# Two transformer layers with experts on one core: order of the first loads, norm factors as rows, scatters bounded to real rows, kept loads behind the first layer's only, one of two row sums moved to VectorE

## The chip, the cores and the metric

The kernel runs on one core of a Trainium2 chip. The metric is the device time of one execution in microseconds (us), lower is better. One execution was profiled; all rows below come from it. Engines are named as the profile names them: PE multiplies matrices (PEld is its weight load, which runs beside it), DVE, ACT and POOL work on elements, SP only issues DMAs here. A "q" behind the name (SPq, ACTq, POOLq) is that engine's own sequencer: the DMAs that it issues.

## The reference

Two layers of a decoder over T = 512 tokens of width D = 1024, fp32. Layer 0 mixes tokens by dilated window attention, layer 1 by stick-breaking attention (16 heads each). Behind each mixer stands a norm, a router that picks 2 of 16 experts for each token, the experts, and a second norm.

```python
for layer in range(DEPTH):
    mixed = mixer_dilated(x, ...) if layer == 0 else mixer_stick_breaking(x, ...)
    x = layer_norm(DEEPNORM_ALPHA * x + mixed, ln1_g[layer], ln1_b[layer])
    ffn = moe_ffn(x, router_w, router_b, exp_w_gate[layer], exp_w_up[layer], exp_w_down[layer])
    x = layer_norm(DEEPNORM_ALPHA * x + ffn, ln2_g[layer], ln2_b[layer])
```

`moe_ffn` gathers the tokens of each expert, computes `(silu(x @ w_gate) * (x @ w_up)) @ w_down`, scales each row by the token's gate and adds it back to the token's row. 512 tokens times 2 are 1024 rows for 16 experts, 64 an expert on average.

## The kernel before

**Products.** Every fp32 product is done as three products of high and low parts (`mm3`, L151 to L153). `split` makes the parts: ACT copies the high one (L143), DVE subtracts for the low one (L145). Weights come from HBM as raw fp32 on SP's queue, in chunks in the order of use, and are split before PE reads them. The tile framework orders the instructions of each engine by a timeline of its own, so an edit at one place can move instructions at others.

**Start.** x is four row blocks of 128 tokens (`xres<-x`, L375). `rows_to_T` (L331) transposes a block on PE, eight 128x128 transposes, and splits it. The first projection multiplies blocks 0 and 1 first, then 2 and 3 (`rest`). `load_router` (L393 to L408) loads the router's weights, its bias, and the factors g and b of the first norm of both layers by six DMAs on ACT's queue; the four of the factors (L400) go element by element, since element k*128+p of a vector must land on partition p. DVE multiplies them into the router's weights (`rwg`, L404) and sums them (L405).

**Kept parts.** While layer 0 runs, the weights of layer 1's projections are split ahead (`split_ahead`, L269) and their parts written back to HBM by POOL (`kept<-raw`, L276). `parts_of` loads them again by SP (`whi<-kept`, `wlo<-kept`, L281). Each such load waits for the expert weights' load issued last (`at["recent"][-1]`) and for the reload of the row blocks behind the experts (`at["read"]`). In layer 1, `prefetch()` queues loads of expert weights ahead from head 12 on (of 16), and the last kept chunk (kept_121, the last quarter of the output projection) stands behind them.

**Experts.** Each expert has 96 slots (CAP). POOL gathers the rows of its tokens (`gather`, L1091, with a bounds check: slots without a token are skipped). `expert_up` and `expert_down` make Y (96 x 1024), and POOL adds it to the tokens' rows in HBM by a scatter (L1127) into `x2_d`. An empty slot is scattered too, to a spare row behind the 512 real ones, which are written once at the start of the layer (`x2_d[T:]`, L1286). Scatters go one behind the other, as each adds to the same tensor. Of the 16 experts 14 are scattered; the last two are added on PE by one-hot products (L1261). SP loads the weights of the experts (1 MB gate, 1 MB up, 1 MB down each) with at most two chunks in flight (`OUTSTANDING`, L227).

**End of a layer.** When the last scatter has landed, SP reads the 512 rows back (`xres<-x_d`, L1222), PE brings each block into PSUM (`take`, L1236) and adds the last two experts, and the norm follows: for each block ACT sums both halves of a row (L1268, a copy with an accumulated sum), DVE makes the mean (L1269), ACT sums squares (L1271), DVE scales and shifts (L1273, L1278). SP's conditional for overflowing experts stands at L1241.

Of the kernel before, what the change touches and what calls it, by code (L numbers as in the profile page):

```python
# [11 lines left out]
F32 = mybir.dt.float32  # L12
# [9 lines left out]
P = 128  # L22
# [48 lines left out]
def trunk_kernel(ctx, tc, A, out):  # L71
# [19 lines left out]
    def bank(pl):  # L91
        return pl.tile([P, 512], F32, name="bank")
# [109 lines left out]
    RM = (2, 4, 5, 2)  # L202
    RY = 2

    def load(i):

        srcs, kind, j = chunks[i]
        if i in raws or kind == "b":
            return
        k = srcs[0].shape[1]  # L210
        if kind == "a":
            raw = rawp.tile([P, 2048], F32, name="raw0")
            raws[i] = [raw[:, :1024], raw[:, 1024:]]
            for half, t in enumerate(raws[i]):
                load_part(t, srcs, half, 2)
            return
        if j < RY:
            pl = pools["ry"]
        else:
            j, ring = (j - RY) % sum(RM), 0  # L220
            while j >= RM[ring]:
                j, ring = j - RM[ring], ring + 1
            pl = pools["rm", ring] if ring else rawp
        raw = pl.tile([P, 2048], F32, name=f"raw{j}" if pl is rawp else "raw") if hasattr(pl, "tile") else             pl[j // 2][:, j % 2]
        recent = at["recent"]
        for part, src in enumerate(srcs):
            ins = sp.dma_start(raw.rearrange("p (s k c) -> p s k c", k=k, s=len(srcs))[:, part], src).ins  # L227

            for before in (at["after"], recent[-OUTSTANDING] if len(recent) >= OUTSTANDING else None):
                if before is not None:  # L230
                    after(ins, before)
        recent.append(ins)
        raws[i] = (raw, k, len(srcs) == 2)
# [35 lines left out]
    def split_ahead():  # L269

        if coming:
            i, part = coming.pop(0)
            raw = rawp.tile([P, 2048], F32, name="raw1")
            load_part(raw[:, 1024:1536], chunks[i][0], part, 4)
            split(raw[:, :512].bitcast(F32R), raw[:, 512:1024].bitcast(F32R), raw[:, 1024:1536])
            pool.dma_start(kept[i][part], raw[:, :1024].rearrange("p (j c) -> p j c", j=2))  # L276

    def parts_of(i, half):
        parts = [splp.tile([P, 1024], F32R, name=f"w{x}") for x in ("hi", "lo")]
        for j, t in enumerate(parts):  # L280
            ins = sp.dma_start(t.bitcast(F32).rearrange("p (q c) -> p q c", q=2),  # L281
                               kept[i][2 * half:2 * half + 2, :, j].rearrange("q p c -> p q c")).ins
            for before in (at["recent"][-1], at["read"]):
                after(ins, before)
        return parts

# [83 lines left out]
    xS = [xp.tile([P, KT, T], F32R, name=f"xT{s}") for s in "hl"]  # L370
    xres = xp.tile([P, 4, D], F32, name="xres")
    for n in range(4):
        if n == 2:
            load_to(1)
        sp.dma_start(xres[:, n, :], x[n * P:(n + 1) * P, :])  # L375

    rest = []
    for n in range(4):
        if n < 2:
            at["begun"] = rows_to_T(*xS, xres[:, n, :], n, streams=True)  # L380
        else:
            rest.append(lambda n=n: rows_to_T(*xS, xres[:, n, :], n, streams=True))


    rb = const.tile([P, NE], F32, name="rb")
# [4 lines left out]
    def load_router():  # L390
        tmp = xp.tile([P, 5, KT * NE], F32, name="tmp", tag="Ol")
        rw = tmp[:, 0].rearrange("p (k e) -> p k e", k=KT)
        gbs = tmp[:, 1, :4 * KT].rearrange("p (j k) -> p j k", j=4)  # L393
        sums = tmp[:, 4, :4 * NE].rearrange("p (j e) -> p j e", j=4)
        with tc.issue_after(at["begun"]):
            act.dma_start(rw, A["router_w"].rearrange("(k p) e -> p k e", p=P))
            act.dma_start(rb, bass.AP(tensor=A["router_b"].tensor, offset=A["router_b"].offset, ap=[[0, P], [1, NE]]))
            for l in range(2):
                for i, name in enumerate(("ln1_g", "ln1_b")):
                    act.dma_start(gbs[:, 2 * l + i], A[name][l].rearrange("(k p) -> p k", p=P))  # L400
        for l in range(2):
            w2 = [rwg[l], tmp[:, 2].rearrange("p (k e) -> p k e", k=KT)]
            for i in range(2):
                tt(w2[i], rw, gbs[:, 2 * l + i, :, None].to_broadcast([P, KT, NE]), op=ALU.mult)  # L404
                dve.tensor_reduce(sums[:, 2 * l + i], w2[i].rearrange("p k e -> p e k"), axis=AX.X, op=ALU.add)  # L405
        ps = bank(psC)[:, :4 * NE]
        pe.matmul(ps, lhsT=ones_r.bitcast(F32), rhs=tmp[:, 4, :4 * NE], start=True, stop=True)
        dve.tensor_copy(gsum.rearrange("p l i e -> p (l i e)"), ps)  # L408
# [699 lines left out]
    def expert_down(mp, hs, Y, wd, gate, x2_d=None, row=None):  # L1108

        pt = bank(psC)[:, :2 * CAP].rearrange("p (k t) -> p k t", k=2)  # L1110
        for k in range(2):
            pe.transpose(pt[:, k, :], hs[:, k * P:(k + 1) * P], ident[:CAP, :CAP])
        hh = mp.tile([P, 2, CAP], F32R, name="hh")
        hl = mp.tile([P, 2, CAP], F32R, name="hl")
        split(hh, hl, pt)
        wd = wd()
        for c in range(2):
            ps = bank(psD)[:CAP]
            for k in range(2):
                mm3(ps, hh[:, k, :], hl[:, k, :], *wd(k, c * 512, (c + 1) * 512), k == 0, k == 1)  # L1120
            if row is None:
                split(*Y, ps, scale=gate, view=lambda t: t[:, c * 512:(c + 1) * 512])
            else:
                act.activation(Y[:, c * 512:(c + 1) * 512], ps, AF.Copy, scale=gate)  # L1124
        if row is None:
            return
        pool.indirect_dma_start(out=x2_d[:, :], out_offset=bass.IndirectOffsetOnAxis(ap=row, axis=0),  # L1127
                                in_=Y, in_offset=None, compute_op=ALU.add)

    def overflow(l, x1_d, x2_d, rt, X, Y, XX):  # L1130

# [33 lines left out]
    def post(l, x1, x2_d, last, done):  # L1165
        with ExitStack() as c:
# [79 lines left out]
            with ExitStack() as c2:  # L1246
                cp = open_pool(c2, f"cp{l}")

                act.activation(cp.tile([P, 1], F32, name="root"), spare1, AF.Sqrt)
                mv = cp.tile([P, 4, 6], F32, name="mv")  # L1250
                st = cp.tile([P, 4, 4], F32, name="st")
                junk = cp.tile([P, D], BF16, name="junk")
                halves = [slice(half * 512, half * 512 + 512) for half in range(2)]
                for n in range(4):
                    if n:
                        take(n)
                    ps, r = sums[n], xres[:, n, :]
                    for i, parts in enumerate(late):
                        for half, cs in enumerate(halves):
                            for j, t in enumerate(parts):  # L1260
                                ins = pe.matmul(ps[half], lhsT=holds[:, i, n * P:(n + 1) * P], rhs=t[:, cs], start=False,  # L1261
                                                stop=i * j == 1, skip_group_check=True).ins
                    if n == 0:
                        with tc.issue_after(ins):
                            load_to(at["load"] + 2)
                            split_to(at["split"] + 2)
                    for half, cs in enumerate(halves):
                        act.activation(junk[:, cs], ps[half], AF.Copy, accum_out=st[:, n, half:half + 1])  # L1268
                    stt(mv[:, n, 0:1], st[:, n, 0:1], st[:, n, 1:2], neg_d, op0=ALU.add, op1=ALU.mult)  # L1269
                    for half, cs in enumerate(halves):  # L1270
                        act.activation(junk[:, cs], ps[half], AF.Square, bias=mv[:, n, 0:1],  # L1271
                                       accum_out=st[:, n, 2 + half:3 + half])
                        stt(r[:, cs], ps[half], mv[:, n, 0:1], g_b[:, cs], op0=ALU.add, op1=ALU.mult)  # L1273
                    if n % 2:
                        tt(mv[:, n - 1:n + 1, 1], st[:, n - 1:n + 1, 2], st[:, n - 1:n + 1, 3], op=ALU.add)  # L1275
                        scale_of(mv[:, n - 1:n + 1], EPS / ALPHA ** 2)
                    for m in (n - 1, n) if n % 2 else ():
                        stt(xres[:, m, :], xres[:, m, :], mv[:, m, 3:4], b_b, op0=ALU.mult, op1=ALU.add)  # L1278
                        done(m, xres[:, m, :])
        return xres  # L1280

    def layer(l, attend, xTs, xres, done):
        last = []

        x2_d = dram.tile([T + P, D], F32, name=f"x2_d{l}")
        sp.dma_start(x2_d[T:], xres[:, 0])  # L1286

        def project_out(qd, Oh, Ol):
            def gen():
# [49 lines left out]
```

## Time and profile before

| | before |
|---|---|
| median of 3 runs (lowest to highest) | 1361.58 us (1356.65 to 1364.33) |
| the profiled execution | 1364.12 us, span 1362.3 us |
| mean granted TensorE clock | 0.954 |
| PE busy | 1247.7 us (92%) |
| DVE, ACT, POOL busy | 899.1, 859.0, 203.4 us |
| DMA moved | 289.60 MB, mean 213 GB/s |
| scatters `x_d<-Y,wr` | 28 issues |

The span is the time from the first to the last instruction, and 1.8 us of the execution lie around it. The page cuts the span into 40 slices of 34 us; a digit is the tenth of a slice that an engine is busy. PEclk is the granted clock of TensorE: 1.00 is the level of 2.4 GHz, 0.50 that of 1.2 GHz, and between them a stretch has some of each. Layer 0's first gathers stand at 654 us and its experts' last stretch at 765 to 821 us; layer 1's last stretch is at 1265 to 1318 us.

### The profile page before, as it was taken

The numbers are of one execution on the slowest core, as the hardware profiler recorded it, in microseconds if no ns is written. First come the engines' busy times: TensorE is split into PE (matmuls) and PEld (weight loads), VectorE is DVE, ScalarE is ACT, GpSimd is POOL, SyncE is SP. The second block draws the span as 40 slices with busy tenths as digits, with TensorE's granted clock in tenths as the row PEclk, the third lists the DMA queues.
The fourth block names the chain that finished last, engine by engine and source line by source line (L and its number), as shares of the span: only waits on it lengthen the run. The fifth ranks groups of instructions, "written<-read, shape, count | busy, mean of one in ns | idle before, by whom it ended". The sixth has DMA issues, their size and how long they took to land. (4 is left out here: it accounts for less than half of the span.)

```text
span 1362.3 us, 19699 instructions
## 1 busy us (share of the span) xinstructions
PE 1247.7 (92%) x6784; PEld 1022.9 (75%) x6784; DVE 899.1 (66%) x1620; ACT 859.0 (63%) x1538; POOL 203.4 (15%) x285
## 2 busy tenths in 40 slices
PE   6999999999999999988799987999999967899876
PEld 5998888789877879877577654988888856677543
DVE  4455665656555645576799774488878857798765
ACT  3356644665356635656699775387778756698664
POOL 3001000011001100010333110022221210332010
PEclk8999999999999999997799999999999977899997
DMA  8865455555455545478699996474444666799982
GB/s 239 284 216 171 155 186 167 178 166 171 147 186 171 164 149 174 158 255 309 226 299 320 312 291 239 132 215 154 156 155 155 218 234 213 249 318 316 288 261 106
DMA packets 176651, 289.60 MB, mean 213 GB/s; under 512 B 17787, under 2 KB 108027, under 8 KB 176540
## 3 DMA queue, kind: packets, MB, share of 16 engines
q1 hardware_dynamic: 153760, 230.72, 51.7%
q0 software_dynamic: 17344, 57.29, 13.5%
q8 instruction: 57, 0.93, 0.3%
q10 hardware_dynamic: 5436, 0.21, 0.3%
q14 instruction: 54, 0.44, 0.1%
HBM read 220.48 MB, written 63.50 MB: 208 GB/s over the span
## 5 line engine op out<-in xcount | busy, mean ns | idle before, releaser
L145 DVE TENSOR_TENSOR wlo<-raw,whi 128x1024 fp32r<-128x1024 f32 x176 | 212.8, 1221 | 94.8 <-ACT whi L143 93.4
L151 PE MATMUL bank<-xTh,whi 128*128 128x512 f32 (+1 forms) x608 | 235.3, 388 | 5.1 <-DVE kl L145 5.1
L152 PE MATMUL bank<-xTl,whi 128*128 128x512 f32 (+1 forms) x608 | 234.2, 385 | 0.0
L153 PE MATMUL bank<-xTh,wlo 128*128 128x512 f32 (+1 forms) x608 | 234.1, 385 | 0.0
L143 ACT ACTIVATE whi<-raw 128x1024 fp32r<-128x1024 f32 x176 | 183.7, 1054 | 67.4 <-PE bank L152 21.1
L145 DVE TENSOR_TENSOR raw<-raw 128x512 fp32r<-128x512 f32 x64 | 44.3, 692 | 141.7 <-ACT raw L143 141.7
L143 ACT ACTIVATE raw<-raw 128x512 fp32r<-128x512 f32 x64 | 40.4, 632 | 152.2 <-DMA raw<-sb_w_in 117.2
L151 PEld LDWEIGHTS bank<-xTh,whi 128*128 128x128 f32 x608 | 116.5, 192 | 24.5 <-issue 5.8
L153 PEld LDWEIGHTS bank<-xTh,wlo 128*128 128x128 f32 x608 | 116.5, 192 | 19.5
L152 PEld LDWEIGHTS bank<-xTl,whi 128*128 128x128 f32 x608 | 117.0, 192 | 18.2
L152 PE MATMUL bank<-wlo,XX 128*96 128x512 f32 x256 | 107.4, 420 | 7.3 <-DVE wlo L145 7.1
L151 PE MATMUL bank<-whi,XX 128*96 128x512 f32 x256 | 106.4, 416 | 7.1 <-ACT whi L143 7.0
L152 PE MATMUL bank<-wlo,xTh 128*128 128x256 f32 x384 | 109.3, 285 | 0.0
L151 PE MATMUL bank<-whi,xTh 128*128 128x256 f32 x384 | 109.1, 284 | 0.0
L153 PE MATMUL bank<-whi,xTl 128*128 128x256 f32 x384 | 109.1, 284 | 0.0
L276 POOL DMA_DIRECT2D kept<-raw x64 | 34.4, 537 | 478.1 <-DVE raw L145 448.5
L153 PE MATMUL bank<-whi,XX 128*96 128x512 f32 x256 | 104.1, 407 | 0.0
L1127 POOL DMA_INDIRECT x_d<-Y,wr x28 | 45.2, 1614 | 201.0 <-ACT Y L1124 139.5
L151 PEld LDWEIGHTS bank<-whi,xTh 128*128 128x128 f32 x384 | 73.7, 192 | 0.5 <-DVE xres L1273 0.2
L152 PEld LDWEIGHTS bank<-wlo,xTh 128*128 128x128 f32 x384 | 73.6, 192 | 0.5
L153 PEld LDWEIGHTS bank<-whi,xTl 128*128 128x128 f32 x384 | 73.3, 191 | 0.1
L629 ACT ACTIVATE Sb<-Sb,st 128x256 f32<-128x256 f32 (+1 forms) x128 | 61.6, 485 | 11.4 <-DVE st L624 11.2
(261 smaller groups left out, 2997.8 us busy)
## 6 DMA issues: line engine op xcount, KB each, us to landing
kept<-raw POOLq DMA_DIRECT2D x64, 512.0 KB, 3.1
raw<-dil_w_in SPq DMA_DIRECT2D x96, 256.0 KB, 4.5
raw<-exp_w_gate SPq DMA_DIRECT2D x32, 512.0 KB, 6.6
raw<-exp_w_up SPq DMA_DIRECT2D x32, 512.0 KB, 7.6
raw<-exp_w_down SPq DMA_DIRECT2D x16, 1024.0 KB, 8.4
whi<-kept SPq DMA_DIRECT2D x32, 512.0 KB, 5.8
wlo<-kept SPq DMA_DIRECT2D x32, 512.0 KB, 5.0
raw<-dil_w_in SPq DMA_DIRECT2D x24, 512.0 KB, 4.6
```

The source lines that it names most:

```text
L143: ins = act.activation(view(hi), src, AF.Copy, scale=scale).ins
L145: tt(view(lo), src, view(hi).bitcast(F32), op=ALU.subtract)
L151: pe.matmul(ps, lhsT=lh, rhs=rh, start=start, stop=False, **kw)
L152: pe.matmul(ps, lhsT=lh, rhs=rl, start=False, stop=False, **kw)
L153: pe.matmul(ps, lhsT=ll, rhs=rh, start=False, stop=stop, **kw)
L276: pool.dma_start(kept[i][part], raw[:, :1024].rearrange("p (j c) -> p j c", j=2))
L629: act.activation(sb[:, b0:, h, :], sb[:, b0:, h, :], AF.Exp, bias=st[:, n, hh, 0:1], scale=-1.0, accum_out=st[:, n, hh, 1:2])
L1127: pool.indirect_dma_start(out=x2_d[:, :], out_offset=bass.IndirectOffsetOnAxis(ap=row, axis=0), in_=Y, in_offset=None, compute_op=ALU.add)
```

## The change

1. **First loads in order of use.** The first chunk's halves are loaded between row blocks 0, 1 and 2 of x instead of together behind block 1.
2. **Norm factors as rows.** The g and b of both layers come as rows of 128 elements on 16 partitions (two DMAs in place of four), and one PE transpose of 32 rows brings them onto the partitions. DVE reads them from PSUM. Loads ahead for layer 1 are issued after the last row block's split.
3. **Scatters without empty slots.** The scatter gets the gather's bounds check, so a slot without a token is skipped; the spare rows of `x2_d` and their write at the start of each layer go.
4. **Kept parts.** The loads of kept parts wait for what the first such load of the program waited for (in layer 0), and for nothing later.
5. **Row sums.** Of the two sums of a block, ACT keeps one, DVE takes the other as a reduction (8 in a run).

```diff
-    def load(i):
+    def load(i, halves=(0, 1)):
...
-            for half, t in enumerate(raws[i]):
-                load_part(t, srcs, half, 2)
+            for half in halves:
+                load_part(raws[i][half], srcs, half, 2)
...
-            load_part(raw[:, 1024:1536], chunks[i][0], part, 4)
+            with tc.issue_after(at["begun"]):
+                load_part(raw[:, 1024:1536], chunks[i][0], part, 4)
...
-            for before in (at["recent"][-1], at["read"]):
+
+            at.setdefault("behind", (at["recent"][-1], at["read"]))
+            for before in at["behind"]:
                 after(ins, before)
...
     for n in range(4):
-        if n == 2:
-            load_to(1)
+        if n in (1, 2):
+            load(0, (n - 1,))
         sp.dma_start(xres[:, n, :], x[n * P:(n + 1) * P, :])
+    at["load"] = 1
...
-            rest.append(lambda n=n: rows_to_T(*xS, xres[:, n, :], n, streams=True))
+            def later(n=n):
+                at["begun"] = rows_to_T(*xS, xres[:, n, :], n, streams=True)
+            rest.append(later)
+    first_rows = at["begun"]
...
-            for l in range(2):
-                for i, name in enumerate(("ln1_g", "ln1_b")):
-                    act.dma_start(gbs[:, 2 * l + i], A[name][l].rearrange("(k p) -> p k", p=P))
+            for i, name in enumerate(("ln1_g", "ln1_b")):
+                act.dma_start(rows[2 * KT * i:2 * KT * (i + 1)], A[name].rearrange("l (k p) -> (l k) p", p=P))
+        with tc.issue_after(at["begun"]):
+            gbs = bank(psC)[:, :4 * KT]
+            pe.transpose(gbs, rows, ident[:4 * KT, :4 * KT])
...
-                                in_=Y, in_offset=None, compute_op=ALU.add)
+                                in_=Y, in_offset=None, compute_op=ALU.add, bounds_check=T - 1, oob_is_err=False)
...
-                    for half, cs in enumerate(halves):
-                        act.activation(junk[:, cs], ps[half], AF.Copy, accum_out=st[:, n, half:half + 1])
+                    act.activation(junk[:, halves[0]], ps[0], AF.Copy, accum_out=st[:, n, 0:1])
+                    dve.tensor_reduce(st[:, n, 1:2], ps[1], axis=AX.X, op=ALU.add)
...
-        x2_d = dram.tile([T + P, D], F32, name=f"x2_d{l}")
-        sp.dma_start(x2_d[T:], xres[:, 0])
+        x2_d = dram.tile([T, D], F32, name=f"x2_d{l}")
```

How the instructions then stand on the engines, at three places. First ACT, some 10 us into the program, before (raw_604 is a load ahead for layer 1, raw_208 the second chunk of layer 0's weights, `xTh<-bank` splits a row block):

```order
L397 DMA rb<-router_b 128x16
L400 DMA tmp<-ln_g 128x8x1
L143 ACTIVATE raw_604<-raw_604 128x512
L400 DMA tmp<-ln_b 128x8x1
L400 DMA tmp<-ln_g 128x8x1
L143 ACTIVATE whi<-raw_208 128x1024
L400 DMA tmp<-ln_b 128x8x1
L143 ACTIVATE xTh<-bank 128x16x32 x2
```

And after:

```order
L405 DMA rb<-router_b 128x16
L407 DMA tmp<-ln_g 16x128
L143 ACTIVATE raw_603<-raw_603 128x512
L407 DMA tmp<-ln_b 16x128
L143 ACTIVATE xTh<-bank 128x16x32
L143 ACTIVATE whi<-raw_207 128x1024
L143 ACTIVATE xTh<-bank 128x16x32
L143 ACTIVATE whi<-raw_207 128x1024
```

Four issues of factors have become two, and the first split of row block 2 stands ahead of the second chunk's instead of behind it. On DVE the multiplications into `rwg` (L404 before, L415 after), which stood between these splits, now stand behind the last of them.

SP in layer 1, from the last heads on, before (qql is scratch of the attention, kept_121 the last kept chunk, rmh, rml and Y are buffers of expert weights):

```order
L471 DMA qql<-raw_11387 64x512 x4
L227 DMA raw_11486<-exp_w_gate 128x1024
L227 DMA raw_11486<-exp_w_up 128x1024
L227 DMA rmh<-exp_w_down 128x2x1024
L227 DMA rmh<-exp_w_gate 128x1024
L227 DMA rmh<-exp_w_up 128x1024
L227 DMA rml<-exp_w_gate 128x1024
L227 DMA rml<-exp_w_up 128x1024
L227 DMA rml<-exp_w_down 128x2x1024
L281 DMA whi<-kept_121 128x2x512
L281 DMA wlo<-kept_121 128x2x512
```

And after:

```order
L482 DMA qql<-raw_11423 64x512 x4
L283 DMA whi<-kept_121 128x2x512
L283 DMA wlo<-kept_121 128x2x512
L228 DMA raw_11522<-exp_w_gate 128x1024
L228 DMA raw_11522<-exp_w_up 128x1024
L228 DMA rmh<-exp_w_down 128x2x1024
L283 DMA whi<-kept_121 128x2x512
L283 DMA wlo<-kept_121 128x2x512
L228 DMA rmh<-exp_w_gate 128x1024
```

The kept chunk has moved from behind eight loads of expert weights to the place ahead of them and among the first three.

DVE at the end of layer 1, the norm's last block, before:

```order
L1273 SCALAR_TENSOR_TENSOR xres<-bank,mv,g_b 128x512
L1278 SCALAR_TENSOR_TENSOR xres<-xres,mv,b_b 128x1024 x2
L1269 SCALAR_TENSOR_TENSOR mv<-st,neg_d 128x1
L1273 SCALAR_TENSOR_TENSOR xres<-bank,mv,g_b 128x512 x2
L1275 TENSOR_TENSOR mv<-st 128x2
```

And after:

```order
L1289 SCALAR_TENSOR_TENSOR xres<-xres,mv,b_b 128x1024 x2
L1284 SCALAR_TENSOR_TENSOR xres<-bank,mv,g_b 128x512
L1279 TENSOR_REDUCE st<-bank 128x1
L1280 SCALAR_TENSOR_TENSOR mv<-st,neg_d 128x1
L1284 SCALAR_TENSOR_TENSOR xres<-bank,mv,g_b 128x512 x2
```

The reduction of the last block stands right ahead of its mean, and one scaling (512 columns) has moved behind the pair of shifts.

## Rows read from the trace of the kernel before

**Rows 1.** The page: span, PE's tenths and clock by slice, POOL's queue (packets, MB, share)
```profile
span 1362.3 us, 19699 instructions
PE   6999999999999999988799987999999967899876
...
PEclk8999999999999999997799999999999977899997
...
q0 software_dynamic: 17344, 57.29, 13.5%
```
**Rows 2.** Windows: us, busy of PE, PEld, DVE, ACT, POOL, clock, DMA share, GB/s
```profile
22.00:28.00 6.00, 0.00 (x0) 0.00 (x0) 2.08 (x4) 3.08 (x4) 0.00 (x0) 0.69 0.82 187
28.00:34.00 6.00, 5.72 (x26) 5.49 (x27) 4.87 (x11) 1.20 (x2) 0.00 (x0) 0.50 0.35 97
34.00:40.00 6.00, 6.00 (x50) 6.00 (x49) 2.28 (x3) 3.19 (x4) 0.00 (x0) 0.95 1.03 373
```
**Rows 3.** Timeline: start, us, engine, line, operation, [idle before <-what ended it]
```profile
19.24 3.43 ACTq L400 DMA_DIRECT2D tmp<-ln_g  x1
...
22.71 1.06 ACT L143 ACTIVATE whi<-raw 128x1024 fp32r<-128x1024 f32 x1 [7.29 <-issue]
...
25.92 0.29 DVE L404 TENSOR_TENSOR rwg<-tmp 128x128 f32<-128x128 f32 x1 [9.78 <-DMA tmp<-ln_g]
...
28.28 1.97 PE L331 MATMUL bank<-ident,xres 128*128 128x128 f32 x8 [6.63 <-DVE xTl L145]
```
**Rows 4.** Windows: layer 1's attention, and two stretches at its end
```profile
860.00:1090.00 230.00, 228.58 (x1346) 203.46 (x1345) 177.94 (x309) 171.61 (x334) 48.22 (x93) 1.00 0.56 175
...
1094.00:1099.00 5.00, 1.19 (x7) 0.82 (x5) 3.81 (x8) 3.45 (x7) 0.00 (x0) 1.00 0.70 242
...
1109.00:1114.00 5.00, 3.39 (x13) 2.80 (x12) 3.90 (x7) 3.88 (x8) 0.00 (x0) 0.50 0.51 163
```
**Rows 5.** Timeline: SP and PE at the end of layer 1's attention
```profile
1088.42 0.38 SPq L227 DMA_DIRECT2D rml<-exp_w_down  x1
...
1094.23 0.38 SPq L281 DMA_DIRECT2D whi<-kept  x1
...
1098.08 0.93 PE L151 MATMUL bank<-whi,Oh 128*128 128x512 f32 x3 [3.81 <-DMA whi<-kept]
```
**Rows 6.** DMA from 765 to 825 us: packets, MB, share of 16 engines; scatters and landing
```profile
q1 hardware_dynamic: 4234, 15.71, 77.9%
q0 software_dynamic: 560, 1.97, 16.9%
...
x_d<-Y,wr POOLq DMA_INDIRECT x5, 9.7
```
**Rows 7.** DMA from 654 to 682 us, gathers alone, four of eight named in the row
```profile
q0 software_dynamic: 785, 1.79, 22.6%
...
X<-x_d,wr POOLq DMA_INDIRECT x4, 7.9
```
**Rows 8.** Windows: the experts' last stretch in layer 0 and in layer 1
```profile
765.00:821.00 56.00, 47.98 (x192) 29.71 (x191) 40.55 (x53) 38.31 (x56) 7.08 (x5) 0.94 0.95 292
...
1265.00:1318.00 53.00, 42.05 (x186) 26.43 (x184) 37.03 (x48) 36.08 (x51) 7.41 (x5) 1.00 0.91 289
```
**Rows 9.** Timeline: behind the last scatter, layer 0 (836) and layer 1 (1325 on)
```profile
836.08 3.18 PE L1236 MATMUL bank<-xres,ident 128*128 128x512 f32 x4 [3.20 <-SPq L1241]
...
1325.06 1.76 SPq L1222 DMA_DIRECT2D xres<-x_d  x4
...
1328.91 3.75 PE L1236 MATMUL bank<-xres,ident 128*128 128x512 f32 x4 [3.59 <-DMA xres<-x_d]
```
**Rows 10.** Group of ACT's sums (1336 to 1362 us); timeline rows of DVE
```profile
L1268 ACT ACTIVATE junk<-bank 128x512 bf16<-128x512 f32 x8 | 4.7, 591 | 1.1 <-PE bank L1261 1.0
...
1089.46 0.67 DVE L791 TENSOR_SCALAR z<-bank 128x512 f32<-128x512 f32 x1
...
1351.76 0.21 DVE L1269 SCALAR_TENSOR_TENSOR mv<-st,neg_d 128x1 f32<-128x1 f32 x1
```

More of the change, by code (lines that the diff above doesn't have):

```diff
@@ L203, in trunk_kernel @@
     RY = 2
-    def load(i):
+    def load(i, halves=(0, 1)):
         srcs, kind, j = chunks[i]
-        if i in raws or kind == "b":
+        if kind == "b" or i in raws and 0 in halves:
             return
@@ L211, in load @@
         if kind == "a":
-            raw = rawp.tile([P, 2048], F32, name="raw0")
-            raws[i] = [raw[:, :1024], raw[:, 1024:]]
-            for half, t in enumerate(raws[i]):
-                load_part(t, srcs, half, 2)
+            if 0 in halves:
+                raw = rawp.tile([P, 2048], F32, name="raw0")
+                raws[i] = [raw[:, :1024], raw[:, 1024:]]
+            for half in halves:
+                load_part(raws[i][half], srcs, half, 2)
             return
@@ L392, in load_router @@
         rw = tmp[:, 0].rearrange("p (k e) -> p k e", k=KT)
-        gbs = tmp[:, 1, :4 * KT].rearrange("p (j k) -> p j k", j=4)
+        rows = tmp[:4 * KT, 1]
         sums = tmp[:, 4, :4 * NE].rearrange("p (j e) -> p j e", j=4)
-        with tc.issue_after(at["begun"]):
+        with tc.issue_after(first_rows):
             act.dma_start(rw, A["router_w"].rearrange("(k p) e -> p k e", p=P))
             act.dma_start(rb, bass.AP(tensor=A["router_b"].tensor, offset=A["router_b"].offset, ap=[[0, P], [1, NE]]))
-            for l in range(2):
-                for i, name in enumerate(("ln1_g", "ln1_b")):
-                    act.dma_start(gbs[:, 2 * l + i], A[name][l].rearrange("(k p) -> p k", p=P))
+            for i, name in enumerate(("ln1_g", "ln1_b")):
[3 more added lines that the diff above has]
+            pe.transpose(gbs, rows, ident[:4 * KT, :4 * KT])
+        gbs = gbs.rearrange("p (i l k) -> p i l k", i=2, l=2)
         for l in range(2):
@@ L403, in load_router @@
             for i in range(2):
-                tt(w2[i], rw, gbs[:, 2 * l + i, :, None].to_broadcast([P, KT, NE]), op=ALU.mult)
+                tt(w2[i], rw, gbs[:, i, l, :, None].to_broadcast([P, KT, NE]), op=ALU.mult)
                 dve.tensor_reduce(sums[:, 2 * l + i], w2[i].rearrange("p k e -> p e k"), axis=AX.X, op=ALU.add)
```

## The prediction, before the changed kernel was run

> **What bounds the kernel now.** I read the slices first. PE is at 9 tenths from the second slice to the nineteenth, and its clock at 9 of 10 nearly all along: the attention stages are bound by PE [rows 1]. Whatever delays PE ahead of them goes to the end in full, since PE has no idle time in which to make it up. The places where PE is below 9 are the first slice, the experts of both layers and the last tail, so I read these by windows and timeline.
>
> At the start PE does nothing from 22 to 28 us, and then runs at the half level: 26 instructions in 6 us, where the next 6 us hold 50 [rows 2]. The timeline gives the cause. ACT executes in order and is held by the issues of the element-wise factors: one issue takes 3.43 us, and the split behind it (22.71) was released by nothing but "issue", after 7.29 us of idling. DVE is held too: its multiplication into `rwg` waits 9.78 us for the factors, and the split of row block 2 stands behind it. PE's transposes come after 6.63 us of waiting for that split [rows 3].
>
> In the experts' last stretches the DMA engines are the bound: 0.95 and 0.91 of their time is taken while PE is busy for 47.98 of 56 and 42.05 of 53 us [rows 8]. Of layer 0's stretch the DMA view says what fills them: weights 77.9%, and POOL's queue, which there holds five scatters, 16.9% [rows 6]. Attention in layer 1 is PE's alone, 228.58 of 230 us at full clock [rows 4].
>
> **The start.** Removed: two of four factor issues, the element-wise form of the rest, and the place of the multiplication ahead of the splits. The gap of 6.63 us goes [rows 3]. With it goes the half level behind it: eight transposes take 1.97 us, which leaves 3.75 us of the window for 18 products, 0.208 us each, against 6.00/50 = 0.12 at the full level [rows 2, 3]. That is 18 x 0.088 = 1.6 us, and about 1.0 for the transposes, if these halve too. So 9.2 us are open. Added: one PE transpose of 32 rows (0.25 us by an eighth of 1.97, at the half level), and the split of row block 2 on ACT and DVE remains ahead of PE. I leave 1.5 us for that and for the second chunk's split, which now stands behind block 2's: **gain 7.5 us**. Bounds: 4 (a third of the gap stays and the clock falls as before) and 10.5 (nothing stays, and the spare rows' write of 512 KB ahead of the first weights is worth 1.4 us by 512 KB at 373 GB/s [rows 2]). The order of x's blocks and the first chunk's halves I cost at nothing: the first products need block 0, block 1 and half 0 in both orders. If that cover is wrong, a half is 512 KB, 1.4 us by the same rate. The four multiplications and four sums are the same instructions; read from PSUM and moved behind the splits, they are beside PE's products, where DVE is busy for 2.28 of 6 us [rows 2].
>
> **Kept loads.** In layer 1 SP issues the last kept chunk at 1094.23, 5.8 us after the last prefetched weights (1088.42), and PE waits 3.81 us for it [rows 5]; in that window it works 1.19 of 5 us, and a little later the clock is at the half level [rows 4]. Now the chunk is issued ahead of the prefetch, some ten us earlier, and DMA has room (share 0.56 [rows 4]). What is displaced is the prefetch, by 2 MB; the prefetched buffers are not needed before the router is done. So 3.8 us go, and of the half level (5 us of it cost 2.5) I take half: **gain 5 us**, bounds 2 (attention's last heads are late next: DVE is busy 3.81 and 3.90 of 5 us in both windows [rows 4]) and 9 (all of the half level goes, and the router's chain with it).
>
> **Scatters.** Five scatters carry 1.97 MB: 5 x 96 rows x 4 KB, so empty slots move as full rows now. They take 16.9% of 60 us, 10.1 us of all 16 engines, 2.03 us each or 0.0211 us a row [rows 6]. On average 64 of 96 slots are real (1024 rows to 16 experts). That the bounds check saves bytes is seen at the gathers, which have it: eight of them carry 1.79 MB, 437 rows of 768 [rows 7]. But they keep 785 packets, 98 for a gather, so a skipped slot isn't free for certain. I take 0.018 to 0.021 us for each of 32 skipped rows, 0.58 to 0.68 us a scatter, 8.1 to 9.5 us for a layer's 14. The weights' chain is the one that is late, and it has some 0.8 of the queues' time (77.9 of 95 in the share [rows 6]): 8.8 x 0.8 = 7.0 us earlier for the last weights. Behind them the last scatter must land before the rows are read back: PE waits 3.20 us for SP in layer 0 and 3.59 us for the rows in layer 1 [rows 9], and a scatter lands 9.7 us after its issue [rows 6], one after another. A third fewer bytes shorten the last by perhaps 0.5, in layer 1 with the half level behind it (3.75 us for four products [rows 9]) by 1.5. **Gain 7.5 us in layer 0, 8.5 in layer 1**; bounds 2 to 11 and 3 to 13. The low ends are what remains if PE, which is busy for 0.86 and 0.79 of these stretches, becomes late soon [rows 8]; the high ends are all 9.5 and half of the wait behind.
>
> **Row sums.** ACT saves 0.59 us a block [rows 10]. That is worth nothing at the end, where DVE's two shifts run until just before the last mean at 1351.76; the reduction now stands ahead of this mean. No row shows it; a DVE operation that reads 128x512 from PSUM takes 0.67 us [rows 10], so the end is 0.67 later. In layer 0, 0.3 of the same. **Loss 1.0 us**; bounds 1.5 lost, or 0.6 gained where ACT's saving counts.
>
> **The rest.** The first heads of layer 1 stand in another order on PE. PE has 1.4 us of idle time in that whole window [rows 4], so a new order can hardly gain and may lose: 0, bounds 2 gained and 3 lost.
>
> **Sum.** 7.5 + 5 + 7.5 + 8.5 - 1.0 = 27.5 us. From the profiled execution (span 1362.3, its own time 1364.12) it gives 1336.6; that execution lies 2.5 above the median of the runs shown, 1361.58, so by the median **1334 us**. The half widths of the bounds (3.3, 3.5, 4.5, 5, 1, 2.5), added as squares, make 8.7: its own range is 1325 to 1343.
>
> **The rivals.**
>
> *A skipped slot keeps half its cost.* For it: the gathers' 98 packets each, nearly as many as the scatters' 112 [rows 6, 7]. Against it: eight gathers take 22.6% of 28 us, 0.79 us each, where a scatter takes 2.03. Then 4.4 us of DMA go instead of 8.8, 3.5 of the chain instead of 7.0, and the tails halve: gains of 3.8 and 4.3, sum 19.6, **1342 us**. The Trainium skill ("DMA: Bandwidth & Descriptors", section on the anatomy of one DMA on the gpsimd path) has a rule on this side: about 2.0 us fixed for a DMA and its bytes at 436 GB/s on top. By it 131 KB less would be 0.30 us a scatter, an estimate, 4.2 us a layer. The 2.03 us of [rows 6] are engine time, not the time to landing, so the trace doesn't yet decide between them.
>
> *The two waits are only exchanged.* PE waits at the start for another operand (block 3, or the factors' transpose in PE's order), and at the end of layer 1 for the last heads; the clock falls as before. Start and kept loads then give 4 and 2 and less: about 18 in all, **1343 us**. For it: DVE is busy 4.87 of the 6 us that follow the gap [rows 2].
>
> *The scatters stay as long as they are*, so that the change doesn't do there what it says: the engines read and write a skipped row all the same. 27.5 - 16 is about 12: **1349.5 us**. The gathers' bytes speak against it [rows 7].
>
> *Slower: the new order of layer 1's first heads.* These heads pass work between PE, ACT and DVE (busy 228.58, 171.61 and 177.94 of 230 us [rows 4]); where the new order makes PE wait for splits, its clock falls to the half level, as it did at 28 us [rows 2]. 10 us at that level cost 5. Beyond 55 us of it, a quarter of this window, the gain of 27.5 is gone; at 70 us the run is at 1334 + 35 = **1369 us**. Against it: 51 us of slack on DVE, and a window that holds the full level now.
>
> **How the numbers follow.** The forecast has 0.60, the half-cost slot 0.14, the exchanged waits 0.09, the unchanged scatters 0.08, the slower heads 0.09 (0.05 beyond 0.5% and 0.04 short of it). About 0.5%, 6.8 us, is what a measurement of this kernel can tell from no change. Of the unchanged scatters I put half within it, since the other terms may come in low too. So faster 0.60 + 0.14 + 0.09 + 0.04 = 0.87, same 0.08, slower 0.05. The range takes in the forecast's own, both rivals next to it and the bounds of the larger terms: 1320 to 1349, which leaves out the last two rivals (0.17) and a little of the forecast.
>
> **What would show it.** Right: no gap of PE at 22 to 28 us and full clock behind it; the last kept loads issued before the last eight weights' loads, no wait of PE for them; POOL's queue at about 53.6 MB instead of 57.3 (28 x 131 KB less [rows 1]), a scatter near 1.4 us of all engines; the experts' last weights 7 us earlier in each layer, measured from the layer's first gather; the last mean 0.7 us later against its block's products. Wrong: a new wait of some us in PE's row at 12 to 30 us, clock below 1.00 between 860 and 1090, or scatters of 2 us with fewer bytes.

## The result, and the profile after

| | before | after |
|---|---|---|
| median of 4 runs each (lowest to highest) | 1359.12 us (1354.37 to 1364.33) | 1345.20 us (1341.04 to 1348.13) |
| the profiled execution | 1364.12 us, span 1362.3 | 1346.51 us, span 1344.7 |
| mean granted clock | 0.954 | 0.959 |

The ratio of the times, after to before, is 0.9895, with a 95% interval of 0.9845 to 0.9944: 13.9 us faster, half of the 27.5 that the sum gave. A later series of eight runs beside other kernels (e5_after) gave 0.9909 (0.9875 to 0.9943). Single executions of one kernel lie as far apart as the whole effect (35 of the kernel before: 1349.33 to 1366.22 us), so single spans are no measure of a term; the terms below are taken inside a stage, or from the series.

The page of the changed kernel, the lines that answer to [rows 1]:

```profile
span 1344.7 us, 19713 instructions
PE   8999999999999999998799987999999987899975
...
PEclk9999999999999999997799998999999987799998
...
q0 software_dynamic: 17344, 53.47, 12.3%
```

POOL's queue carries 3.8 MB less in the same 17344 packets. The first slice is at 8 where it was at 6.

**The start** came as described. The windows after, which answer to [rows 2] (columns as there), and ACT's two issues of the factors, which answer to [rows 3]:

```profile
22.00:28.00 6.00, 5.75 (x46) 5.28 (x45) 4.22 (x11) 1.39 (x3) 0.00 (x0) 1.00 0.78 243
28.00:34.00 6.00, 6.00 (x53) 6.00 (x52) 3.95 (x5) 3.27 (x5) 0.00 (x0) 1.00 1.04 387
```

```profile
14.02 0.47 ACTq L407 DMA_DIRECT2D tmp<-ln_g  x1
...
14.62 0.35 ACTq L407 DMA_DIRECT2D tmp<-ln_b  x1
```

The two windows hold 99 PE instructions where they held 26, all at the full level. The 73 more are worth 73 x 0.12 = 8.8 us by the later windows' 0.12 us each. The two issues of factors take 0.47 and 0.35 us; the costliest of the four before took 3.43.

But at 84 us a wait stands that was not there, on the timeline of the changed kernel (start, us, engine, line, [idle before <-what ended it]):

```profile
81.41 0.63 ACT L143 ACTIVATE raw<-raw 128x512 fp32r<-128x512 f32 x1 [4.60 <-DMA raw<-sb_w_in]
...
83.37 0.50 ACT L640 ACTIVATE Sb<-Sb,st 128x256 f32<-128x256 f32 x1
...
84.01 0.33 PE L645 MATMUL bank<-ident,Sb 128*128 128x128 f32 x1 [1.85 <-ACT Sb L640]
```

ACT, in order, waits 4.60 us for a load that is needed only in layer 1; attention's first exponential (L640) stands behind it, and PE behind that. The two windows around it:

```profile
76.00:86.00 10.00, 8.03 (x37) 6.48 (x38) 5.10 (x14) 5.40 (x14) 0.66 (x2) 0.96 0.35 133
86.00:96.00 10.00, 10.00 (x55) 8.85 (x54) 4.76 (x13) 5.60 (x14) 0.53 (x1) 0.87 0.44 143
```

PE idles 2.0 us, and the clock's 0.96 and 0.87 cost 0.4 and 1.3 more: 3.7 us of the 8.8 are given back there. Before, ACT waited for such loads until 80.85 and 88.43 us, the second time right ahead of the exponential, while PE, which was later, still had other products to do:

```profile
75.00:85.00 10.00, 10.00 (x83) 9.91 (x83) 3.83 (x6) 3.76 (x6) 0.53 (x1) 1.00 1.10 304
85.00:95.00 10.00, 10.00 (x56) 8.65 (x55) 7.08 (x23) 6.86 (x22) 0.53 (x1) 1.00 0.55 186
```

**The kept loads** are issued at 1069.66, and the waits of PE at the end of layer 1's attention no longer name them. SP's row and all waits of PE from 1070 to 1120 us, which answer to [rows 5] (columns: what waited for what: us in total, times, longest):

```profile
1069.66 0.54 SPq L283 DMA_DIRECT2D whi<-kept  x1
```

```profile
PE bank L859 <- ACT ah L143: 5.3, 3, 1.9
PE bank L151 <- DVE osum L868: 1.4, 1, 1.4
PE bank L859 <- DVE al L145: 0.5, 2, 0.3
```

A stretch at the half level remains behind them: the clock is 0.50 from 1099 to 1104 us.

**The experts** are where the sum failed. The weights' chain of layer 0, from the first issue of `rmx<-exp_w_down` to the last issue of any `exp_w_down`, before and after:

```profile
670.39 0.38 SPq L227 DMA_DIRECT2D rmx<-exp_w_down  x1
...
812.81 0.38 SPq L227 DMA_DIRECT2D raw<-exp_w_down  x1
```

```profile
662.16 0.38 SPq L228 DMA_DIRECT2D rmx<-exp_w_down  x1
...
803.67 0.38 SPq L228 DMA_DIRECT2D raw<-exp_w_down  x1
```

142.4 us have become 141.5, and the other executions with all slots scattered in the old order have 139.0 to 139.6 (e1_start, e3_kept, e4_sums). Yet the scatters did shrink, as the last stretch after shows (755 to 811 us, windows and DMA, which answer to [rows 6, 8]):

```profile
755.00:811.00 56.00, 48.60 (x207) 30.78 (x206) 41.83 (x54) 38.29 (x54) 7.08 (x5) 0.97 0.91 292
```

```profile
q1 hardware_dynamic: 4035, 15.04, 78.9%
q0 software_dynamic: 556, 1.27, 11.7%
...
x_d<-Y,wr POOLq DMA_INDIRECT x5, 8.4
```

Five scatters carry 1.27 MB (62 rows each) in 11.7% of 56 us, 1.31 us of all engines a scatter where it was 2.03: 0.0211 us for a row that moves, as before, and nothing measurable for a skipped one. The DMA share fell from 0.95 to 0.91, and the weights came no sooner. Most of the freed DMA time was left idle.

**The end of layer 1.** The rows come back at 1308.71, 5.6 us after the last scatter's issue (10.0 before), and PE's first product is at the full level; these answer to [rows 9]:

```profile
1303.09 1.41 POOL L1138 DMA_INDIRECT x_d<-Y,wr  x1 [10.08 <-DVE wlo L145]
...
1308.71 1.76 SPq L1233 DMA_DIRECT2D xres<-x_d  x4
...
1312.29 1.96 PE L1247 MATMUL bank<-xres,ident 128*128 128x512 f32 x4 [2.84 <-DMA xres<-x_d]
```

These are two single executions. From the last scatter's issue to the reload, the four kernels that scatter all slots in the old order have 7.4 to 10.0 us, the three that bound the scatters 5.6 to 7.2 (the changed kernel, e2_scatter, e5_after).

**The row sums.** DVE's reduction takes 0.68 us and stands right ahead of the last mean, which answers to [rows 10] (first the last product before, then the rows after):

```profile
1349.16 0.40 PE L1261 MATMUL bank<-Yl,XX 96*128 96x512 f32 x1
```

```profile
1331.17 0.40 PE L1272 MATMUL bank<-Yl,XX 96*128 96x512 f32 x1
...
1333.60 0.68 DVE L1279 TENSOR_REDUCE st<-bank 128x1 f32<-128x512 f32 x1
...
1334.38 0.22 DVE L1280 SCALAR_TENSOR_TENSOR mv<-st,neg_d 128x1 f32<-128x1 f32 x1
```

The mean comes 3.21 us after the last product's start; before, that product's start was at 1349.16 and the mean at 1351.76, 2.60 later. That is 0.61 lost.

A second loss goes with this part, at the start of layer 1. The ten us that begin 28.5 us behind the reload of the rows, before and after:

```profile
850.00:860.00 10.00, 9.02 (x74) 8.37 (x73) 8.29 (x17) 3.82 (x10) 0.00 (x0) 1.00 0.13 54
```

```profile
840.50:850.50 10.00, 7.42 (x42) 6.08 (x42) 8.90 (x19) 3.92 (x11) 0.00 (x0) 0.83 0.01 2
```

The clock's 0.83 costs 1.7 us. At this place the clock is 0.83 to 0.86 in all eight kernels here that have part 5, e4_sums with part 5 alone among them, and 1.00 in the six without. PE's waits there have moved: 2.0 us for `xTl` after and 1.0 before, 0.3 us for `xres` after and 1.1 before.

### The profile page after: what moved, and what is told of

Read it like the earlier page. It is cut to its first block, busy times and chain, and to the rows that moved or that the text cites. A ratio compares the mean times of both kernels' runs of the same rounds, so it can differ in the third digit from the quotient of the medians.

```text
span 1344.7 us, 19713 instructions
## 1 busy us (share of the span) xinstructions
PE 1241.7 (92%) x6785; PEld 1019.1 (76%) x6785; DVE 904.6 (67%) x1628; ACT 853.5 (63%) x1522; POOL 200.3 (15%) x285
## 3 DMA queue, kind: packets, MB, share of 16 engines
q0 software_dynamic: 17344, 53.47, 12.3%
## 5 line engine op out<-in xcount | busy, mean ns | idle before, releaser
L151 PE MATMUL bank<-whi,XX 128*96 128x512 f32 x256 | 105.1, 411 | 4.9 <-ACT whi L143 4.8
L153 PE MATMUL bank<-whi,XX 128*96 128x512 f32 x256 | 102.7, 401 | 0.0
L640 ACT ACTIVATE Sb<-Sb,st 128x256 f32<-128x256 f32 (+1 forms) x128 | 61.7, 485 | 11.8 <-DVE st L635 11.7
```

The source lines that it names most:

```text
L151: pe.matmul(ps, lhsT=lh, rhs=rh, start=start, stop=False, **kw)
L153: pe.matmul(ps, lhsT=ll, rhs=rh, start=False, stop=stop, **kw)
L640: act.activation(sb[:, b0:, h, :], sb[:, b0:, h, :], AF.Exp, bias=st[:, n, hh, 0:1], scale=-1.0, accum_out=st[:, n, hh, 1:2])
```

## The experiments

### One part at a time

The first four kernels are the kernel before with one part each.

**e1_start:** the edits of `load`, `load_router` and the first loop over x, as in the diff above.

> The kernel before with parts 1 and 2 alone (first loads in order of use, norm factors as rows; the spare rows' write stays). The prediction's term: 7.5 us faster than before, bounds 4 to 10.5. The trace of the changed kernel has the layer's first stored rows (x_d<-xq) 10.6 us earlier, so a second theory expects the upper end, 9 to 11. The rival 'waits are only exchanged' expects 4 or less, with a gap of PE between 12 and 30 us.

Measured 0.9953 (0.9928 to 0.9978), 6.4 us faster, with bounds of 3.0 and 9.8. The gap at 22 us is gone, and the return near 84 us is there but smaller: PE waits 1.4 us for L638's exponential, and the clock stays at 1.00. The forecast's 7.5 lies in the interval, the second theory's 9 to 11 only with its lower end. The rival's 4 or less touches the interval, but its gap of PE between 12 and 30 us is not there.

**e2_scatter:**

```diff
-                                in_=Y, in_offset=None, compute_op=ALU.add)
+                                in_=Y, in_offset=None, compute_op=ALU.add, bounds_check=T - 1, oob_is_err=False)
...
-        x2_d = dram.tile([T + P, D], F32, name=f"x2_d{l}")
-        sp.dma_start(x2_d[T:], xres[:, 0])
+        x2_d = dram.tile([T, D], F32, name=f"x2_d{l}")
```

> The kernel before with part 3 alone (bounded scatters, no spare rows). The prediction's terms: 16 us faster, 7.5 and 8.5 in the two layers, with the weights' chain behind the experts 7 us shorter in each. A second theory, from the changed kernel's trace: the chain from the first rmx<-exp_w_down issue to the last exp_w_down issue of layer 0 went only from 142.4 to 141.5 us, so the freed DMA time doesn't reach the weights; then 1 to 3 us a layer there, and 2 to 8 us in all with what the last scatter's landing gives.

Measured 0.9958 (0.9932 to 0.9984), 5.7 us faster (2.2 to 9.2), not 16. The chain of layer 0's weights is 141.6 us (issues at 673.01 and 814.61), not 7 shorter. The second theory holds.

**e3_kept:**

```diff
-            for before in (at["recent"][-1], at["read"]):
+            at.setdefault("behind", (at["recent"][-1], at["read"]))
+            for before in at["behind"]:
```

> The kernel before with part 4 alone (kept parts' loads behind the first layer's only). The prediction's term: 5 us faster, bounds 2 to 9, no wait of PE for whi<-kept. Rival: the 3.8 us are only exchanged for a wait on the last heads, 0 to 2 us faster.

Measured 0.9940 (0.9915 to 0.9966), 8.1 us faster (4.6 to 11.5). The forecast's 5 lies in the interval, the rival's 0 to 2 does not.

**e4_sums:**

```diff
-                    for half, cs in enumerate(halves):
-                        act.activation(junk[:, cs], ps[half], AF.Copy, accum_out=st[:, n, half:half + 1])
+                    act.activation(junk[:, halves[0]], ps[0], AF.Copy, accum_out=st[:, n, 0:1])
+                    dve.tensor_reduce(st[:, n, 1:2], ps[1], axis=AX.X, op=ALU.add)
```

> The kernel before with part 5 alone (one of two row sums on DVE). The prediction's term: 1 us slower, bounds 1.5 slower to 0.6 faster. Rival, from the changed kernel's tail: the two sums of a block go side by side, so each block's mean comes about 0.6 us earlier and the end is 0 to 2 us earlier. Either is below what the runs tell apart; the tail behind the last row block's products in the trace decides.

Measured 1.0002 (0.9976 to 1.0028). At the end the trace decides for the prediction: last product's start and last mean are 3.21 us apart, as in the changed kernel.

```profile
1340.29 0.40 PE L1261 MATMUL bank<-Yl,XX 96*128 96x512 f32 x1
...
1343.50 0.22 DVE L1269 SCALAR_TENSOR_TENSOR mv<-st,neg_d 128x1 f32<-128x1 f32 x1
```

The four add up to 19.9 us, each with 3.5 us either way; the whole measured 12.4 and 13.9. So they add up at best roughly: the 6.0 to 7.5 us that are missing are about what the four errors, added as squares, allow (7).

### Why freed DMA time did not reach the weights

Three theories stood: the sum of all engines' time decides (the prediction's), two chunks in flight set the pace, or the busiest DMA engine decides. The next four ran beside one another.

**e5_after:** the changed kernel as it is.

> The changed kernel once more, beside the next three on the same chip: 14 us faster than before, as in its first runs; scatters near 1.3 us of all 16 engines, the chain of the experts' weights in layer 0 (first rmx<-exp_w_down issue to last exp_w_down issue) near 141.5 us.

Measured 0.9909 (0.9875 to 0.9943). The chain of layer 0's weights is 142.8 us here, 141.5 in the first profiled execution.

**e6_spread:** tokens of an expert go to other rows of its 96; the number of instructions doesn't change.

```diff
-            full = [P, 2 * (n1 - n0), CAP]
-            tt(ph, slot[:, None, :].to_broadcast(full), pos.rearrange("p n c -> p (n c)")[:, :, None].to_broadcast(full),
-               op=ALU.is_equal)
+            full = [P, 2 * (n1 - n0), 16, CAP // 16]
+            tt(ph.rearrange("p m (a b) -> p m a b", a=16),
+               slot.rearrange("p (b a) -> p a b", a=16)[:, None].to_broadcast(full),
+               pos.rearrange("p n c -> p (n c)")[:, :, None, None].to_broadcast(full), op=ALU.is_equal)
```

> The changed kernel with the slots of an expert in another order: token number s of an expert goes to row 6*(s mod 16) + s div 16 of the 96, so that its empty slots lie spread over the rows instead of all at the end. Theory 'engines': the 96 rows are dealt to the 16 DMA engines in order, six to each, so empty slots at the end relieve only the last engines while a weight load, spread over all 16, ends as late as before; spread out, each engine has two rows less and the weights' chain of a layer is 5 to 9 us shorter: 10 to 16 us faster than the changed kernel. Theory 'sum' (the prediction's, all engines' time together decides): no difference to the changed kernel, within 3 us. Theory 'in flight' (two chunks in flight set the pace): no difference either.

Measured 0.9794 (0.9748 to 0.9841), 1329.64 us: 16.7 us faster than the changed kernel beside it, a little above the 10 to 16 of theory "engines", with the same bytes and packets. The chain of layer 0's weights and the last stretch (745 to 801 us):

```profile
661.51 0.38 SPq L228 DMA_DIRECT2D rmx<-exp_w_down  x1
...
792.70 0.38 SPq L228 DMA_DIRECT2D raw<-exp_w_down  x1
```

```profile
745.00:801.00 56.00, 54.23 (x258) 37.53 (x256) 48.32 (x62) 45.80 (x65) 8.52 (x6) 1.00 0.96 306
```

131.2 us instead of 141.5, a DMA share of 0.96 instead of 0.91, and PE busy for 54.23 us instead of 48.60 (both windows end some 8 us behind the last scatter's issue; this one holds six scatters, the other five). Theory "engines" forecast this and the two others forecast no difference. That the rows are dealt to the engines six by six in order is inferred from that effect and from the 112 packets of a scatter (16 times 7); no view here shows single engines.

**e7_no_rows:** in this kernel no row is scattered, so 14 experts' sums are left out of the result.

```diff
+            self.away = spare.bitcast(I32)
+            ts(self.away, ps, 0.0, float(T), op0=ALU.mult, op1=ALU.add)
...
-                        expert_down(mp, h_last, Y[:, e % 4], weights, rt.gate[:, e - 2:e - 1], x2_d, rt.wr[:, e - 2:e - 1])
+                        expert_down(mp, h_last, Y[:, e % 4], weights, rt.gate[:, e - 2:e - 1], x2_d, rt.away[:, e - 2:e - 1])
```

> The changed kernel with every slot of every scatter out of bounds, so that no row is moved (the 14 experts' sums are left out of the result); issues and queue entries stay. By the share of POOL's queue the rows take 1.3 us of all engines a scatter, 18 us a layer. If DMA time bounds the experts' last stretch: 10 to 15 us less a layer, limited by PE at 9.2 us an expert. If two chunks in flight set the pace: under 4 us a layer.

Measured 0.9664 (0.9606 to 0.9722), 1313.4 us, 33 us below the changed kernel: 16 a layer, a little above the range for "DMA time bounds it". DMA view, 745 to 801 us:

```profile
q1 hardware_dynamic: 4411, 16.32, 80.1%
q0 software_dynamic: 673, 0.00, 0.7%
...
x_d<-Y,spare POOLq DMA_INDIRECT x6, 5.0
```

673 entries without data take 0.7% of 56 us, 0.4 us for six scatters: a skipped slot costs next to nothing, and the rows that move are what costs DMA time. But a scatter without rows still lands 5.0 us behind its issue, where the changed kernel's take 8.4. So this kernel shortens the scatters' own chain as well as the weights', and does not tell the two apart.

**e8_three:**

```diff
-OUTSTANDING = 2
+OUTSTANDING = 3
```

> The changed kernel with three chunks of expert weights in flight instead of two. Theory 'in flight': the weights' chain of a layer is 5 to 10 us shorter and DMA share in the last stretch rises to 0.97 or more. Theories 'engines' and 'sum': within 4 us of the changed kernel, each load's time to landing longer by half.

Measured 0.9909 (0.9878 to 0.9940), the same as the changed kernel. But the chain of weights did become shorter, 121.8 us:

```profile
660.86 0.38 SPq L228 DMA_DIRECT2D rmx<-exp_w_down  x1
...
782.64 0.38 SPq L228 DMA_DIRECT2D raw<-exp_w_down  x1
```

While these loads run the DMA share is 0.98 in the old order too, as theory "in flight" forecast, and PE is never idle:

```profile
734.00:790.00 56.00, 56.00 (x276) 39.99 (x275) 52.16 (x68) 51.35 (x74) 11.81 (x7) 1.00 0.98 343
```

So two in flight do hold the loads back, and with a third the engines' time is used. But lifting the limit gives the run nothing, since another thing is late. POOL's scatters in this kernel:

```profile
730.14 1.82 POOL L1138 DMA_INDIRECT x_d<-Y,wr  x1 [1.63 <-ACT whi L143]
...
740.23 2.05 POOL L1138 DMA_INDIRECT x_d<-Y,wr  x1 [2.54 <-DMA x_d<-Y,wr]
750.20 1.43 POOL L1138 DMA_INDIRECT x_d<-Y,wr  x1 [7.92 <-ACT sg L1114]
...
803.16 1.41 POOL L1138 DMA_INDIRECT x_d<-Y,wr  x1 [4.36 <-issue]
```

From 730 to 790 us they are 9 to 11 us apart, each about its issue and landing (8.5 us median there), and the last one is issued at 803.16, as in the changed kernel (803.55). That the chain of scatters is the bound in this kernel is read from these rows, not tested; three chunks in flight with the spread order were not run.

### Which of it is the order, and the new wait

**e9_order_only:** the edit of e6_spread on the kernel before.

> The kernel before with the slots in the spread order alone, scatters unbounded: every one of the 96 rows still moves, so each DMA engine has the same six. Theory 'engines': no difference to before, within 4 us, since the order matters only where empty slots are skipped (the gathers, which skip already, are few at a time). If the order helped by itself, the run would be 8 us or more faster.

Measured 0.9937 (0.9912 to 0.9962), 8.5 us faster (5.2 to 11.9; 5.8 by the medians), which the theory did not expect. What the order can change in that kernel is the gathers, which skip empty slots there. The chain of layer 0's weights is 138.0 us (issues at 664.27 and 802.30), just below what single executions of kernels in the old order gave (139 to 143). Where the 8.5 us lie stays open.

**e10_part3_spread:** e2_scatter and e6_spread on the kernel before.

> The kernel before with part 3 (bounded scatters) and the spread order. Theory 'engines': part 3 alone gave about 6 us, the order 17 on top of the changed kernel, so 20 to 24 us faster than before, and a chain of the experts' weights near 131 us in both layers. The prediction's terms for part 3 were 16 us.

Measured 0.9853 (0.9814 to 0.9891), 20.0 us faster, where part 3 in the old order gave 5.7. The chain is 130.6 us (663.79 to 794.34). Against e9_order_only, with the order the same, bounded scatters are worth 11.5 us, with some 6 either way, which takes in the prediction's 16.

By the runs alone, then, the order is worth 8.5 us with all slots scattered and 16.7 with bounded scatters, and these two are not far apart for their errors. The traces part them. From a layer's first gather to the reload of its rows, both layers together, in us, one profiled execution for each kernel:

| | old order | spread order |
|---|---|---|
| all 96 rows scattered | 335.2, 335.3, 331.1, 332.7 (before, e1_start, e3_kept, e4_sums) | 330.6 (e9_order_only) |
| bounded scatters | 327.8, 330.5, 334.1 (after, e5_after, e2_scatter) | 308.0, 305.5, 304.7, 308.9 (e6_spread, e10_part3_spread, e11_late_ahead, e12_spread_again) |

In this stage the order gives some 24 us where the scatters skip slots, and where they do not it stays within what the others differ by. So the gain of e6_spread lies in the experts' stages, and most of the 8.5 us of e9_order_only does not, as far as one execution shows.

**e11_late_ahead:** in the changed kernel with the spread order, the splits ahead come behind attention's first exponential. The fifth and sixth call make no split, which puts two of them off, and the loads ahead no longer wait for the row blocks.

```diff
+        at["calls"] = at.get("calls", 0) + 1
-        if coming:
+        if coming and at["calls"] not in (5, 6):
...
-            split(raw[:, :512].bitcast(F32R), raw[:, 512:1024].bitcast(F32R), raw[:, 1024:1536])
+            with tc.issue_after(at.get("soft", at["begun"])):
+                split(raw[:, :512].bitcast(F32R), raw[:, 512:1024].bitcast(F32R), raw[:, 1024:1536])
...
+                            at.setdefault("soft", ins)
```

> The changed kernel in the spread order, with two splits ahead for layer 1 put off: the ACT instructions that split the weights loaded ahead (raw<-raw) come behind the first exponential of layer 0's attention. In the changed kernel one of them stands ahead of that exponential on ACT and waits some 4.6 us for its load, while PE then waits for the exponential and falls to the half level for 3.4 us near 85 us. Theory: that wait is where a part of the start's gain is given back; without it PE's 500th product comes 2 to 4 us earlier and the run is 2 to 4 us faster than e12_spread_again. Rival: the time goes to the DVE or the next split, no difference.

**e12_spread_again:** e6_spread once more, beside it.

> The changed kernel in the spread order once more, beside the last: near 1330 us, 26 to 30 us faster than before; PE's wait for the first exponential near 84 us as before.

Measured 0.9771 (0.9734 to 0.9807) for e11_late_ahead and 0.9758 (0.9723 to 0.9793) for e12_spread_again, 1326.39 and 1325.26 us: no difference (and the second is 32 us faster than before, more than the 26 to 30 expected). The wait is gone (first row, e11_late_ahead; second, e12_spread_again):

```profile
76.00:86.00 10.00, 10.00 (x65) 9.04 (x64) 6.34 (x18) 6.64 (x15) 0.53 (x1) 1.00 0.48 127
```

```profile
76.00:86.00 10.00, 7.59 (x39) 6.03 (x38) 5.83 (x14) 4.85 (x10) 1.06 (x2) 1.00 0.40 134
```

PE's 500th product comes at 90.54 us in the first and at 93.73 in the second, 3.2 us earlier, as expected; but e6_spread, the same kernel as the second, has it at 90.86, so this too is within what executions differ by. Small waits of PE stand earlier instead, 0.60 us at 59 and 0.38 and 0.25 us at 71 us in the first. That the wait at 84 us took 3.7 us from the start is read from the rows; that it cost the run as much is not shown.

## Why the prediction held its sign and range, and lost half its size

The measured 1345.2 us lie outside the forecast's own 1325 to 1343. The stated range held because it also took in the two rivals next to it, and neither of them is what happened: that is luck.

**The start** was right in kind, and nearly in size: 8.8 us came where 9.2 were counted open and 7.5 forecast. The step that was missing is what comes next on ACT: the forecast looked for a new wait between 12 and 30 us, and it came at 84. The series gives 6.4 us.

**The kept loads** were right: forecast 5, measured 8.1 (4.6 to 11.5), and the wait went without a new one in that place.

**The row sums** were right at the end of layer 1: 0.67 forecast, 0.61 read. The term lacks the 1.7 us of lower clock at the start of layer 1; the series (3.8 us slower to 3.3 faster) can tell neither from nothing.

**The scatters** carry the miss: forecast 16 us, measured 5.7 (2.2 to 9.2). Their shrinking was sized well, 0.72 us of all engines a scatter against 0.58 to 0.68. What failed is the step "8.8 x 0.8 = 7.0 us earlier for the last weights", which shares a saving on 16 engines out as if they were one: the chain of layer 0's weights became 0.9 us shorter (142.4 to 141.5). A load of weights is done when its last engine is done. (The Trainium skill says so on "DMA: Bandwidth & Descriptors", section "Why a DMA increments its semaphore by 16 and not by 1": the engines of one DMA finish independently, and only all of them mean that the data landed; a tile of 96 partitions is cut over all 16. e6_spread fits this, with a chain 10 us shorter for the same bytes, though no view here shows single engines.) With the empty slots at the end of the 96, some engines would be relieved wholly and the others not at all. That the order of the rows decides is shown: bounded scatters shorten the experts' stages by some 3 us in the old order and by some 24 in the spread one. That uneven engines are the reason is inferred, and the limit of two loads in flight has its part: with three, the engines are busy for 0.98 of the time in the old order too (e8_three). The mean DMA share of 0.95, on which the step rested, can't show this. Of the 5.7 us, the earlier landing of the last scatter in layer 1, some 2 us by the kernels with and without part 3, is the part that the traces show.

**The rivals.** The half-cost slot gave 1342 us, near the time measured, but by luck, as its reason is wrong: skipped slots cost next to nothing (e7_no_rows, and 0.0211 us a row as before). By the Trainium skill's rule (the page "DMA: Bandwidth & Descriptors", section "Anatomy of one DMA — SWDGE (gpsimd) path") a scatter would be 0.30 us shorter for 131 KB, an estimate. The traces don't show these 0.30 us: the median time to landing is 8.2 us before and after over the whole run, and in layer 0's last stretch it fell from 9.7 to 8.4. The engines' time fell by 0.72 us a scatter, and the run followed none of these. Unchanged scatters are refuted by 53.47 MB. The slower heads came, but small. In the same stretch of layer 1's first heads, before and after:

```profile
940.00:960.00 20.00, 18.58 (x95) 14.79 (x94) 19.50 (x35) 17.17 (x35) 5.21 (x11) 1.00 0.32 109
```

```profile
930.00:950.00 20.00, 18.23 (x89) 14.93 (x87) 18.18 (x33) 17.11 (x36) 4.69 (x12) 0.91 0.48 145
```

PE waits 0.86, 0.48 and 0.42 us for splits at 942 to 945 us, and the clock of 0.91 costs 1.8 us; from 992 to 1080 us it is 1.00. That is the clock below 1.00 between 860 and 1090 which the prediction named as a sign of being wrong. Four of the seven kernels with all five parts have it at this place (0.91), and none of those with fewer, so the four single parts leave it out. Of exchanged waits one came, at a place that the rival did not name.

One sentence of the change's description was too strong: loads ahead are not issued later, as the first stands at the same place in SP's order as before, at 5.85 us instead of 7.22.

**The version to keep** is the changed kernel with the spread order: 1329.6 and 1325.3 us in two series, 0.9794 and 0.9758 of the kernel before.

## What to carry to other kernels

A mean DMA share near 1 says that the engines together are full, not that each has the same to do: where some of a transfer's rows are skipped, look which engines they fall on, and spread them before counting the saving. When a stall at the start goes, the engine that was held runs into the next in-order queue: follow it to the first instruction there that waits for something not yet needed. And where a limit on loads in flight may hide another chain, lifting the limit can shorten the loads and not the run (e8_three: 20 us off the loads, nothing off the run).

## What was not expected of the hardware

The order of an expert's tokens among its 96 rows, with bytes and packets unchanged, is worth 16.7 us of 1346 (e5_after against e6_spread). A skipped slot keeps its entry in the queue and takes next to no time: 673 entries took 0.7% of 56 us. A scatter that moves no row at all still takes 5.0 us to land (e7_no_rows). And the order was worth 8.5 us (5.2 to 11.9) even where only the gathers skip slots, which no stage of the trace explains.
